# A hybrid GLA and retention trunk on one core: the retention heads' norm moved in part from VectorE to ScalarE, and token sums spread over other steps

## The chip, the cores and the metric

The kernel runs on one core of a Trainium2 chip. The metric is device time in microseconds, the median over runs. The engines that matter are TensorE (PE in the profile, with its weight loads as PEld), VectorE (DVE), ScalarE (ACT), GpSimd (POOL) and SyncE (SP). Each runs its own list of instructions in order and waits for the others by semaphores. SP issues most weight loads from DRAM; POOL issues those that add onto data already loaded, and some small ones.

## The reference

256 tokens of width 2048 pass a gated linear attention layer (4 heads), a retention layer (8 heads) and a final norm, all float32. The change touches the retention layer's norm of each head, the lines from `mu` on:

```python
def retention_mixer(h, positions, w_in, gn_g, gn_b, w_out):
    proj = h @ w_in
    q, k, v, gate = jnp.split(proj, [RET_DK, 2 * RET_DK, 2 * RET_DK + D_INNER], axis=-1)
    ...
    q, k = apply_rotary(q, cos, sin), apply_rotary(k, cos, sin)
    def step(state, inp):
        qb, kb, vb = inp
        scores = jnp.einsum('bhtk,bhsk->bhts', qb, kb) * dmat
        intra = jnp.einsum('bhts,bhsv->bhtv', scores, vb)
        inter = jnp.einsum('bhtk,bhkv->bhtv', qb, state) * xi
        new_state = g_chunk * state + jnp.einsum('bhsk,bhsv->bhkv', kb * zeta, vb)
        return new_state, intra + inter
    ...
    mu = jnp.mean(o, axis=-1, keepdims=True)
    var = jnp.mean(jnp.square(o - mu), axis=-1, keepdims=True)
    o = ((o - mu) * lax.rsqrt(var + EPS)).reshape(B, S, D_INNER).astype(h.dtype)
    o = o * gn_g + gn_b
    return (o * jax.nn.silu(gate)) @ w_out
```

A head's `o` is 256 tokens by 512, `gn_g` and `gn_b` are vectors of 512 for each head, and mean and variance are one number for each token.

## The kernel before

**Weights.** The weights come in pieces of 128x1024 floats (512 KB), each loaded by SP into one of eight `raw` buffers. A piece is split into a high half `hi` (a ScalarE copy to the reduced format that TensorE multiplies fast, L292) and a low half `lo` (VectorE, raw minus high, L293), with four buffers each; the splits run three pieces ahead of their use (`LOOK = 3`). A product is three matmuls: left high by weight high, left high by weight low, left low by weight high (L416, L417 and L418 in the products, L389 and L390 in the query and key steps). TensorE thus waits for a high half from ScalarE, then for a low half from VectorE, which needs the high half.

**Products of a head.** For the value and gate parts of the weights the tokens are taken in two halves, and a scheme of products P1 to P8 on sums of weights and sums of tokens replaces some of the plain ones. Its steps are named in a string for each head; `q` are query and key pieces, `v` and `g` plain value and gate pieces, `P` the products (two weight pieces each, P1a and P1b say), and `z` marks where sums of weights change:

```python
MIXED = "q0 q1 P1 q2 q3 q4 z P5 q5 P6 q6 q7 P2 P3 v4 v5 v6 P7 v7 g4 g5 P8 g6 g7"
SPREAD = "q0 q1 P1 q2 q3 P2 q4 z P5 q5 P6 q6 q7 P3 v4 v5 v6 P7 v7 g4 g5 P8 g6 g7"
```

Heads 2 and 6 follow SPREAD, the odd heads MIXED, heads 0 and 4 take all q first. The weight sums are made in place in `raw`: once both high and low half of a piece of P1, P6 or P3 have been taken, POOL issues a DMA that adds another weight block onto the buffer (L301, `accum_op=ADD`). What P3's pieces become so is P7's weights.

**The head's other work.** `ret_tasks` is a generator that is stepped once at most of the next steps' ends, so a head's rotary, scores, output `o`, norm and transposes run while the next head's products do. Its norm: ScalarE copies `o` out of PSUM while it sums (L1263) and squares it with the mean as bias while it sums (L1267); VectorE adds the mean (which is held negated) and multiplies by `gg` (L1271), turns the variance into an inverse root with an integer start and three Newton steps on 128x2 numbers (`rsqrt`, L514 to L522), multiplies by it and adds `gb` (L1283), and multiplies by the gate `sg` (in the helper `tt`, L1219). TensorE then transposes the result (L725) and ScalarE and VectorE split it into `ogt`. The gate is a SiLU on ScalarE (L1409). Where ScalarE goes from one function's table to that of another set, a table load (ACT_TABLE_LOAD) stands ahead of the instruction.

**Token sums.** For the output projection the sums of tokens over `ogt` are needed. `make_sums` (L473) builds them in five parts in heads 2 and 6, one part at each named step's end, on VectorE and ScalarE; half of them are then spilled to DRAM by two 512 KB DMAs of POOL (`spill_sums`, L456) and read back in heads 3 and 7 (`back_sums`). Before, the parts stand at the ends of q3, P2, q4, P5 and q5, with the spill behind the last.

**The order.** The tile framework's scheduler simulates the program and sets each engine's order from it, with what `keep` marks held in the order of the program and what stands under `tc.high_priority()` preferred. So a change in the code moves other instructions too.

Of the kernel before, what the change touches and what calls it, by code (L numbers as in the profile page):

```python
# [10 lines left out]
F32 = mybir.dt.float32  # L11
# [3 lines left out]
AF = mybir.ActivationFunctionType  # L15
ALU = mybir.AluOpType

P = 128
# [4 lines left out]
GW = 512  # L23
# [147 lines left out]
def kernel(  # L171
# [17 lines left out]
    nc = tc.nc  # L189
# [11 lines left out]
    gn_p = pool("gn", 3)  # L201
    st_p = pool("st", 4)
# [7 lines left out]
    keep = tc.keep_in_program_order  # L210
# [303 lines left out]
    def rsqrt(y, m, n, name):  # L514
        s = st_p.tile([P, 4, n], F32, tag="nw", name=f"{name}_nw")
        a, b = s[:, 0, :], s[:, 1, :]
        nc.vector.tensor_scalar(a.bitcast(I32), m.bitcast(I32), 1, None, ALU.logical_shift_right)
        nc.vector.tensor_scalar(b.bitcast(I32), a.bitcast(I32), -1, 0x5F3759DF, ALU.mult, ALU.add)
        for it in range(3):
            nc.vector.scalar_tensor_tensor(a, b, -0.5, m, ALU.mult, ALU.mult)  # L520
            nc.vector.tensor_tensor(a, a, b, ALU.mult)
            nc.vector.scalar_tensor_tensor(y if it == 2 else b, a, 1.5, b, ALU.add, ALU.mult)  # L522
# [185 lines left out]
    def o_mms(sc, v, ps):  # L708
        for t in range(2):
            steps = [(0, 0)] if t == 0 else [(0, 1), (1, 2)]  # L710
            for n, (s, blk) in enumerate(steps):
                ah = sc[:, 0, blk * P : (blk + 1) * P]
                al = sc[:, 1, blk * P : (blk + 1) * P]
                end = n == len(steps) - 1
                mm(ps[t], ah, v[:, s, 0, :], start=n == 0, stop=False)
                mm(ps[t], ah, v[:, s, 1, :], start=False, stop=False)
                mm(ps[t], al, v[:, s, 0, :], start=False, stop=end)
# [22 lines left out]
    def split_scores(sc32, sc):  # L740
        nc.scalar.activation(sc[:, 0, :], sc32, AF.Copy)
        nc.vector.tensor_tensor(sc[:, 1, :], sc32, sc[:, 0, :].bitcast(F32), ALU.subtract)
# [474 lines left out]
    def ret_tasks(h, qk, r, r2, box):  # L1217

        tt = lambda *x: keep(nc.vector.tensor_tensor(*x))  # L1219
        a = t4_p.tile([P, 4, SEQ], F32, tag="t4", name=f"ra{h}")  # L1220
        b = t4_p.tile([P, 4, SEQ], F32, tag="t4", name=f"rb{h}")
        tb = lambda i, n: trig[:, i : i + 1, :].to_broadcast([P, n, SEQ])
        four = lambda x: x.rearrange("p (a two) t -> p a two t", two=2)
        tt(a, qk, tb(0, 4), ALU.mult)
        dm = sc_p.tile([P, 384], F32, tag="dm", name=f"dm{h}", bufs=1)
        nc.gpsimd.dma_start(dm, dmat[h])
        yield
        tt(four(b)[:, :, 0, :], four(qk)[:, :, 1, :], tb(1, 2), ALU.mult)
        tt(four(b)[:, :, 1, :], four(qk)[:, :, 0, :], tb(1, 2), ALU.mult)
        gg = gn_p.tile([P, GW], F32, tag="gn", name=f"gg{h}")  # L1230
        gb = gn_p.tile([P, GW], F32, tag="gn", name=f"gb{h}")
        nc.gpsimd.dma_start(gg, gn_g[h * GW : (h + 1) * GW].partition_broadcast(P))
        nc.gpsimd.dma_start(gb, gn_b[h * GW : (h + 1) * GW].partition_broadcast(P))
        yield
        tt(four(a)[:, :, 0, :], four(a)[:, :, 0, :], four(b)[:, :, 0, :], ALU.subtract)
        tt(four(a)[:, :, 1, :], four(a)[:, :, 1, :], four(b)[:, :, 1, :], ALU.add)
        yield
        qs = t4_p.tile([P, 2, 2, SEQ], F32R, tag="t4", name=f"rqs{h}")
        ks = t4_p.tile([P, 2, 2, P], F32R, tag="t4", name=f"rks{h}")
        for dst, src in ((qs, a[:, 0:2, :]), (ks, a[:, 2:4, 0:P])):  # L1240
            nc.scalar.activation(dst[:, 0], src, AF.Copy)
            tt(dst[:, 1], src, dst[:, 0].bitcast(F32), ALU.subtract)
        ps = mis_p.tile([P, 384], F32, tag="mis", name=f"rs{h}")
        for kt in range(2):
            mm(ps[:, 256:384], a[:, 2 + kt, P:SEQ], a[:, kt, P:SEQ], start=kt == 0, stop=kt == 1)
        for kt in range(2):
            mm(ps[:, 0:256], ks[:, 0, kt, :], qs[:, 0, kt, :], start=kt == 0, stop=False)
            mm(ps[:, 0:256], ks[:, 0, kt, :], qs[:, 1, kt, :], start=False, stop=False)
            mm(ps[:, 0:256], ks[:, 1, kt, :], qs[:, 0, kt, :], start=False, stop=kt == 1)
        yield  # L1250
        s32 = sc_p.tile([P, 384], F32, tag="s32", name=f"rs32_{h}", bufs=1)
        sc = sc_p.tile([P, 2, 384], F32R, tag="sc", name=f"rsc{h}")
        with tc.high_priority():
            tt(s32, ps, dm, ALU.mult)
            split_scores(s32, sc)
        yield
        po = [mis_p.tile([P, GW], F32, tag="mis", name=f"ro{h}_ps{t}") for t in range(2)]
        o_mms(sc, box["v"], po)
        o = o_p.tile([P, 2, GW], F32, tag="o", name=f"ro{h}")
        mv = st_p.tile([P, 2, 2], F32, tag="mv", name=f"mv{h}")  # L1260
        with tc.high_priority():
            for t in range(2):
                nc.scalar.activation(o[:, t, :], po[t], AF.Copy, accum_out=mv[:, 0, t : t + 1])  # L1263
            nc.vector.tensor_scalar(mv[:, 0, :], mv[:, 0, :], -1.0 / GW, None, ALU.mult)
            for t in range(2):
                mean = mv[:, 0, t : t + 1]
                nc.scalar.activation(po[t], o[:, t, :], AF.Square, bias=mean, accum_out=mv[:, 1, t : t + 1])  # L1267
        yield
        with tc.high_priority():
            for t in range(2):  # L1270
                keep(nc.vector.scalar_tensor_tensor(o[:, t, :], o[:, t, :], mv[:, 0, t : t + 1], gg, ALU.add, ALU.mult))  # L1271
        yield
        m = st_p.tile([P, 2], F32, tag="m", name=f"rm{h}")
        hr = st_p.tile([P, 2], F32, tag="hr", name=f"ra_{h}")
        with tc.high_priority():
            tt(m, mv[:, 1, :], r2, ALU.mult)
            nc.vector.tensor_scalar(m, m, 1.0 / GW, EPS, ALU.mult, ALU.add)
            rsqrt(hr, m, 2, f"rh{h}")
            tt(hr, hr, r, ALU.mult)
        yield  # L1280
        with tc.high_priority():
            for t in range(2):
                keep(nc.vector.scalar_tensor_tensor(o[:, t, :], o[:, t, :], hr[:, t : t + 1], gb, ALU.mult, ALU.add))  # L1283
        yield
        with tc.high_priority():
            for t in range(2):
                tt(o[:, t, :], o[:, t, :], box["sg"][:, t, :], ALU.mult)
        yield
        yield from transpose_out(
            lambda t, j: o[:, t, j * P : (j + 1) * P], (h % 4) * 4, None, ogt, f"rot{h}"  # L1290
        )
# [11 lines left out]
    def ret_head(h):  # L1303
# [8 lines left out]
        r, r2 = r2_[:, 0, :], r2_[:, 1, :]  # L1312
        box = {}
# [21 lines left out]
        def tile_of(key, pool_, shape, dtype, name):  # L1335
            def get():
                if key not in box:
                    box[key] = pool_.tile(shape, dtype, tag=key, name=name)
                return box[key]

            return get

        v = tile_of("v", v_p, [P, 2, 2, GW], F32R, f"rv{h}")
        sg = tile_of("sg", sg_p, [P, 2, GW], F32, f"rsg{h}")
        o = tile_of("o", o_p, [P, 2, GW], F32, f"re{h}")
# [5 lines left out]
        making = make_sums(ogt, f"rsum{h}", sums_apart, "next_s") if h % 4 == 2 else None  # L1351

        def turn(tok):
            n = toks.index(tok)
            if making and tok in ("q3", "P2", "q4", "P5", "q5"):
                next(making)
                if tok == "q5":
                    spill_sums(f"rsum{h}")
            if last and tok == "v7":
                get_resid(f"resid{h}")  # L1360
            if n == drain:
                while tasks:
                    step()
                if mixed:
                    tasks.append(ret_tasks(h, box["qk"], r, r2, box))
            elif n < drain:
                if tok != "q7":
                    step()
            elif mixed:
                if tok not in ("P7", "g4", "g5"):  # L1370
                    step()
                if last and tok == "g7":
                    back_sums(f"rsum{h}")
            elif tok == "P8":
                tasks.append(ret_tasks(h, box["qk"], r, r2, box))
            elif tok in ("g6", "g7"):
                step()
# [211 lines left out]
```

## Time and profile before

| | |
|---|---|
| median of 3 runs | 1388.78 us (1388.77 to 1391.09) |
| the profiled execution's own time | 1387.9 us |
| its span | 1386.1 us |
| mean granted TensorE clock | 0.997 |
| PE busy | 1366.5 us (99%) |
| DVE busy | 1104.1 us (80%) |
| ACT busy | 851.7 us (61%) |
| POOL busy | 145.5 us (10%) |

The span is the trace's, from the first instruction to the last; the run's own time holds 1.8 us more around it. In rows of a timeline the columns are start, duration, engine, line, operation, output<-inputs, shapes, count, and in brackets the idle time before and what ended it. In the groups they are count, busy time, mean ns of one, and idle time before with what ended most of it. Matmul rows overlap: what one costs is read from start to start. Table loads count as ScalarE's busy time.

### The profile page before, as it was taken

How to read it: one execution, taken by the hardware profiler on the slowest of the kernel's cores; microseconds unless marked ns; L12 is line 12 of the kernel's file. 1: busy time of each engine (PE TensorE's matmuls, PEld its weight loads, DVE VectorE, ACT ScalarE, POOL GpSimd, SP SyncE). 2: the span in 40 equal slices, each digit the busy share in tenths (PEclk: the TensorE clock that was granted, in tenths of full speed). 3: DMA queues.
4: the chain of work that ended last, by engine and by line, in shares of the span. 5: the costliest groups of instructions: out<-in, count | busy, mean ns of one | idle time of the engine just before them, and what ended most of it. 6: DMA issues, size and time to landing. Idle time of an engine off the chain costs nothing.

```text
span 1386.1 us, 18745 instructions
## 1 busy us (share of the span) xinstructions
PE 1366.5 (99%) x6736; PEld 1151.6 (83%) x6736; DVE 1104.1 (80%) x1521; ACT 851.7 (61%) x1118; POOL 145.5 (10%) x206
## 2 busy tenths in 40 slices
PE   9999999999999999999999998999999999999997
PEld 7888888888888888887888897888888889788887
DVE  6686795987878887778888896889858898788883
ACT  6576656655567747565666665666556666566662
POOL 1003020110021021001011010101100101010100
PEclk9999999999999999999999999999999999999999
DMA  9765556789659658758897878898898786879881
GB/s 358 248 178 166 175 167 182 168 244 353 192 152 278 182 174 216 286 162 259 278 301 201 254 210 248 208 335 231 247 367 254 193 275 185 257 195 303 236 289 66
DMA packets 85950, 321.36 MB, mean 232 GB/s; under 512 B 9936, under 2 KB 10960, under 8 KB 84320
## 3 DMA queue, kind: packets, MB, share of 16 engines
q1 hardware_dynamic: 66768, 240.55, 49.9%
q0 software_dynamic: 17648, 72.23, 25.3%
q10 hardware_dynamic: 1440, 7.38, 1.4%
q8 instruction: 53, 0.87, 0.2%
q14 instruction: 41, 0.34, 0.1%
HBM read 307.53 MB, written 12.58 MB: 231 GB/s over the span
## 4 chain that ended last, share of the span: by engine, by line
PE 77%; issue 13%; DMA 6%; DVE 2%; POOL 1%; ACT 1%; POOLq 0%; DVEq 0%; SPq 0%; ACTq 0%
DMA raw<-in_w_all 6%; PE rqk_ps L389 5%; PE re_ps L417 5%; PE re_ps L418 5%; PE re_ps L416 5%; PE gqk_ps L389 4%; PE gg_ps L333 3%; PE gv_ps L334 3%; PE gv_ps L333 3%; PE gv_ps L330 3%; PE gg_ps L330 3%; PE gg_ps L334 3%; PE rqk_ps L390 2%; PE ge_ps L417 2%; PE ge_ps L416 2%
## 5 line engine op out<-in xcount | busy, mean ns | idle before, releaser
L293 DVE TENSOR_TENSOR lo<-raw,hi 128x1024 fp32r<-128x1024 f32 (+1 forms) x569 | 687.8, 1222 | 216.4 <-ACT hi L292 203.9
L292 ACT ACTIVATE hi<-raw 128x1024 fp32r<-128x1024 f32 (+1 forms) x569 | 597.8, 1057 | 392.0 <-DMA raw<-in_w_all 65.8
L301 POOL DMA_DIRECT2D raw<-in_w_all x96 | 83.0, 865 | 552.7 <-DVE lo L293 318.9
L417 PE MATMUL re_ps<-lo,xhl 128*128 128x512 f32 x352 | 137.8, 392 | 0.0
L418 PE MATMUL re_ps<-hi,xhl 128*128 128x512 f32 x352 | 136.9, 390 | 0.0
L416 PE MATMUL re_ps<-hi,xhl 128*128 128x512 f32 x352 | 133.1, 392 | 0.0
L389 PE MATMUL rqk_ps<-xhl,hi 128*128 128x512 f32 x360 | 123.3, 397 | 0.0
L390 PE MATMUL rqk_ps<-xhl,lo 128*128 128x256 f32 x360 | 93.7, 282 | 0.0
L389 PEld LDWEIGHTS rqk_ps<-xhl,hi 128*128 128x128 f32 x360 | 66.7, 188 | 13.3
L416 PEld LDWEIGHTS re_ps<-hi,xhl 128*128 128x128 f32 x352 | 66.4, 189 | 13.5
L418 PEld LDWEIGHTS re_ps<-hi,xhl 128*128 128x128 f32 x352 | 66.2, 188 | 13.4
L417 PEld LDWEIGHTS re_ps<-lo,xhl 128*128 128x128 f32 x352 | 66.3, 188 | 13.1
L389 PE MATMUL gqk_ps<-xhl,hi 128*128 128x512 f32 x216 | 76.5, 398 | 0.0
L333 PE MATMUL gg_ps<-lo,xhl 128*128 128x512 f32 x192 | 75.4, 393 | 0.0
L333 PE MATMUL gv_ps<-lo,xhl 128*128 128x512 f32 x192 | 75.2, 392 | 0.0
L330 PE MATMUL gv_ps<-hi,xhl 128*128 128x512 f32 x192 | 75.0, 393 | 0.0
L334 PE MATMUL gv_ps<-hi,xhl 128*128 128x512 f32 x192 | 75.0, 391 | 0.0
L334 PE MATMUL gg_ps<-hi,xhl 128*128 128x512 f32 x192 | 74.9, 390 | 0.0
L330 PE MATMUL gg_ps<-hi,xhl 128*128 128x512 f32 x192 | 74.8, 391 | 0.0
L390 PEld LDWEIGHTS rqk_ps<-xhl,lo 128*128 128x128 f32 x360 | 66.0, 189 | 2.7
L847 POOL TENSOR_TENSOR s<-s,m 128x64 f32<-128x64 f32 x56 | 36.1, 676 | 232.9 <-DVE m L838 223.6
L390 PE MATMUL gqk_ps<-xhl,lo 128*128 128x256 f32 x216 | 59.0, 280 | 0.0
(447 smaller groups left out, 2859.5 us busy)
## 6 DMA issues: line engine op xcount, KB each, us to landing
raw<-in_w_all SPq DMA_DIRECT2D x447, 512.0 KB, 4.9
raw<-in_w_all POOLq DMA_DIRECT2D x96, 512.0 KB, 7.4
resid<-in_x_n SPq DMA_DIRECT2D x2, 1024.0 KB, 10.2
gg<-in_gn_g POOLq DMA_DIRECT2D x8, 256.0 KB, 4.7
resid_x<-resid ACTq DMA_DIRECT2D x1, 2048.0 KB, 8.9
gb<-in_gn_b POOLq DMA_DIRECT2D x8, 256.0 KB, 4.7
gb_resid<-resid_x POOLq DMA_DIRECT2D x1, 2048.0 KB, 11.7
resid_g<-gb_resid ACTq DMA_DIRECT2D x1, 2048.0 KB, 9.7
```

The costliest lines, as they stand in the source:

```text
L292: a = nc.scalar.activation(hi[:, sl], src[:, sl], AF.Copy)
L293: b = nc.vector.tensor_tensor(lo[:, sl], src[:, sl], hi[:, sl].bitcast(F32), ALU.subtract)
L301: nc.gpsimd.dma_start(raws[n], block(key), accum_op=ALU.add)
L330: first_mm = mm(ps, xh, hi[:, q, :], start=kt == 0, stop=False)
L333: mm(ps, xh, lo[:, q, :], start=False, stop=False)
L334: mm(ps, xl, hi[:, q, :], start=False, stop=kt == NKT - 1)
L389: mm(ps[c], wh, rhs[:, kt, :, :], start=kt == 0, stop=False)
L390: mm(ps[c][:, 0, :], wl, rhs[:, kt, 0, :], start=False, stop=False)
L416: mm(ps, xh, hi[:, q, :], start=start, stop=False, **again)
L417: mm(ps, xh, lo[:, q, :], start=False, stop=False, **again)
L418: mm(ps, xl, hi[:, q, :], start=False, stop=stop, **again)
L847: nc.gpsimd.tensor_tensor(dst, dst, side_of(m[:, li, :], z), ALU.add)
```

## The change

*The norm.* The inverse root's start comes from ScalarE. The inverse root, times the token's scale, and its product with the negated mean become scale and bias of a ScalarE pass over each token half of `o` (L1286, `AF.Identity`). `gg`, `gb` and the gate are then applied by three VectorE passes over both token halves at once (128x1024, in the helper `tt`) in place of six of 128x512. *The token sums.* The five parts stand at the ends of q3, q4, q5, P6 and q6, the spill behind q6.

```diff
@@ -1227,10 +1227,10 @@
-        gg = gn_p.tile([P, GW], F32, tag="gn", name=f"gg{h}")
-        gb = gn_p.tile([P, GW], F32, tag="gn", name=f"gb{h}")
-        nc.gpsimd.dma_start(gg, gn_g[h * GW : (h + 1) * GW].partition_broadcast(P))
-        nc.gpsimd.dma_start(gb, gn_b[h * GW : (h + 1) * GW].partition_broadcast(P))
+        gg = gn_p.tile([P, 1, GW], F32, tag="gn", name=f"gg{h}")
+        gb = gn_p.tile([P, 1, GW], F32, tag="gn", name=f"gb{h}")
+        nc.gpsimd.dma_start(gg[:, 0], gn_g[h * GW : (h + 1) * GW].partition_broadcast(P))
+        nc.gpsimd.dma_start(gb[:, 0], gn_b[h * GW : (h + 1) * GW].partition_broadcast(P))
@@ -1266,25 +1266,33 @@
         yield
-        with tc.high_priority():
-            for t in range(2):
-                keep(nc.vector.scalar_tensor_tensor(o[:, t, :], o[:, t, :], mv[:, 0, t : t + 1], gg, ALU.add, ALU.mult))
-        yield
         m = st_p.tile([P, 2], F32, tag="m", name=f"rm{h}")
-        hr = st_p.tile([P, 2], F32, tag="hr", name=f"ra_{h}")
+        hr = st_p.tile([P, 2, 2], F32, tag="hr", name=f"ra_{h}")
+        nw = st_p.tile([P, 4, 2], F32, tag="nw", name=f"rh{h}_nw")
+        a_, b_ = nw[:, 0, :], nw[:, 1, :]
         with tc.high_priority():
             tt(m, mv[:, 1, :], r2, ALU.mult)
             nc.vector.tensor_scalar(m, m, 1.0 / GW, EPS, ALU.mult, ALU.add)
-            rsqrt(hr, m, 2, f"rh{h}")
-            tt(hr, hr, r, ALU.mult)
+            keep(nc.scalar.activation(a_, m, AF.Ln))
+            keep(nc.scalar.activation(b_, a_, AF.Exp, scale=-0.5))
         yield
         with tc.high_priority():
+            nc.vector.scalar_tensor_tensor(a_, b_, -0.5, m, ALU.mult, ALU.mult)
+            tt(a_, a_, b_, ALU.mult)
+            nc.vector.scalar_tensor_tensor(b_, a_, 1.5, b_, ALU.add, ALU.mult)
+            tt(hr[:, 0, :], b_, r, ALU.mult)
+            tt(hr[:, 1, :], hr[:, 0, :], mv[:, 0, :], ALU.mult)
             for t in range(2):
-                keep(nc.vector.scalar_tensor_tensor(o[:, t, :], o[:, t, :], hr[:, t : t + 1], gb, ALU.mult, ALU.add))
+                nc.scalar.activation(
+                    o[:, t, :], o[:, t, :], AF.Identity, bias=hr[:, 1, t : t + 1], scale=hr[:, 0, t : t + 1]
+                )
         yield
         with tc.high_priority():
-            for t in range(2):
-                tt(o[:, t, :], o[:, t, :], box["sg"][:, t, :], ALU.mult)
+            keep(tt(o, o, gg.to_broadcast([P, 2, GW]), ALU.mult))
+            keep(tt(o, o, gb.to_broadcast([P, 2, GW]), ALU.add))
+        yield
+        with tc.high_priority():
+            tt(o, o, box["sg"], ALU.mult)
         yield
@@ -1352,9 +1360,9 @@
-            if making and tok in ("q3", "P2", "q4", "P5", "q5"):
+            if making and tok in ("q3", "q4", "q5", "P6", "q6"):
                 next(making)
-                if tok == "q5":
+                if tok == "q6":
                     spill_sums(f"rsum{h}")
```

The built programs hold 16 table loads on ScalarE before and 38 after: of the 22 more, eight stand ahead of the logarithms, eight ahead of the exponentials and six ahead of SiLUs that follow them. The order on the engines moves at three places.

On POOL in head 2, before: `raw_6830` and `raw_6842` are the buffers that P6's pieces leave to an added block, `raw_7014` and `raw_7051` those of P3, which P7 reads, and `dm` is the next mask of the scores.

```order
L301 DMA raw_6830<-in_w_all 128x1024
L301 DMA raw_6842<-in_w_all 128x1024
L456 DMA rsum_kept<-rsum_t_7301 128x1024
L456 DMA rsum_kept<-rsum_t_7302 128x1024
L301 DMA raw_7014<-in_w_all 128x1024
L301 DMA raw_7051<-in_w_all 128x1024
L1226 DMA dm_8002<-in_dmat 128x384
```

The same place after the change, where `raw_7003` and `raw_7039` are P3's buffers:

```order
L301 DMA raw_6824<-in_w_all 128x1024
L301 DMA raw_6836<-in_w_all 128x1024
L301 DMA raw_7003<-in_w_all 128x1024
L301 DMA raw_7039<-in_w_all 128x1024
L456 DMA rsum_kept<-rsum_t_7342 128x1024
L456 DMA rsum_kept<-rsum_t_7343 128x1024
L1226 DMA dm_7984<-in_dmat 128x384
```

The two spills have moved from ahead of P3's added blocks to behind them; head 6 is the same.

On ScalarE from head 2 into head 3, before: `ro` is head 2's output, `rsg_7109` its gate, `hi_7655` and `hi_7698` are P1's two pieces of head 3 and `hi_7721` is that of q2.

```order
L292 ACTIVATE hi_7635<-raw_7474 128x1024
L1263 ACTIVATE ro_7626,mv_7627<-ro_ps_7615 128x512
L1263 ACTIVATE ro_7626,mv_7627<-ro_ps_7616 128x512
L1267 ACTIVATE ro_ps_7615,mv_7627<-ro_7626,mv_7627 128x512
L1267 ACTIVATE ro_ps_7616,mv_7627<-ro_7626,mv_7627 128x512
L292 ACTIVATE hi_7655<-raw_7507 128x1024
L1409 ACTIVATE rsg_7109<-rsg_7109,r_109 128x512
L1409 ACTIVATE rsg_7109<-re_ps_7084,r_109 128x512
L292 ACTIVATE hi_7698<-raw_7519 128x1024
L292 ACTIVATE hi_7721<-raw_7573 128x1024
```

After the change P1's pieces are `hi_7648` (it stands ahead of these rows) and `hi_7681`, and `hi_7704` is q2's:

```order
L1267 ACTIVATE ro_ps_7604,mv_7615<-ro_7614,mv_7615 128x512
L1417 ACT_TABLE_LOAD
L1417 ACTIVATE rsg_7097<-re_ps_7072,r_109 128x512
L292 ACTIVATE hi_7681<-raw_7507 128x1024
L1417 ACTIVATE rsg_7097<-rsg_7097,r_109 128x512
L1276 ACT_TABLE_LOAD
L1276 ACTIVATE rh_nw<-rm_7639 128x2
L1277 ACT_TABLE_LOAD
L1277 ACTIVATE rh_nw<-rh_nw 128x2
L1286 ACTIVATE ro_7614<-ro_7614,ra_7640 128x512 x2
L292 ACTIVATE hi_7704<-raw_7561 128x1024
```

Three table loads, the logarithm, the exponential and the two passes over `ro` now stand between P1's pieces and q2's high half.

On TensorE in P3 and P2 of head 1, which take turns there, before: `hi_6691` and `lo_6692` are P3's second piece, `hi_6630` is P2's.

```order
L418 MATMUL re_ps_6690<-hi_6630,xhl 128x512
L416 MATMUL re_ps_6547<-hi_6691,sums 128x512
L416 MATMUL re_ps_6749<-hi_6702,xhl 128x512
L417 MATMUL re_ps_6547<-lo_6692,sums 128x512
L418 MATMUL re_ps_6547<-hi_6691,sums 128x512
```

After the change `hi_6653` and `lo_6654` are P3's first piece, `hi_6685` its second and `hi_6604` P2's:

```order
L417 MATMUL re_ps_6542<-lo_6654,sums 128x512
L418 MATMUL re_ps_6542<-hi_6653,sums 128x512
L416 MATMUL re_ps_6542<-hi_6685,sums 128x512
L416 MATMUL re_ps_6684<-hi_6604,xhl 128x512
L417 MATMUL re_ps_6684<-lo_6605,xhl 128x512
L418 MATMUL re_ps_6684<-hi_6604,xhl 128x512
```

The first matmul of P3's second piece stood behind P2's and now stands ahead of them, right behind P3's first piece; head 5 is the same.

## The prediction

> **What bounds the kernel now.** I read the page first, for which engine has no slack.
>
> ```profile
> span 1386.1 us, 18745 instructions
> PE 1366.5 (99%) x6736; PEld 1151.6 (83%) x6736; DVE 1104.1 (80%) x1521; ACT 851.7 (61%) x1118; POOL 145.5 (10%) x206
> ```
>
> TensorE is the bound: 99% busy. VectorE and ScalarE have a fifth and more of the span free, so work added to or taken from them counts only where TensorE waits for them. So the second view is TensorE's waits (total, times, longest, in us), all of them.
>
> ```profile
> PE re_ps L416 <- ACT hi L292: 3.9, 4, 1.3
> PE re_ps L417 <- DVE lo L293: 3.0, 4, 0.8
> PE warm_ps L551 <- POOL warm L549: 1.8, 1, 1.8
> PE gqk_ps L377 <- ACT hi L292: 1.2, 1, 1.2
> PE gbe_ps L416 <- DVE gb_resid L1036: 0.3, 1, 0.3
> PE gae_ps L417 <- DVE lo L293: 0.3, 1, 0.3
> ```
>
> Only the first two are in the retention heads: eight waits, 6.9 us. The timeline puts them at product P7 of heads 2 and 6 (two waits for a high half, two for a low half in each). Head 2:
>
> ```profile
> 836.88 0.39 PE L417 MATMUL re_ps<-lo,xhl 128*128 128x512 f32 x1
> 837.10 0.39 PE L418 MATMUL re_ps<-hi,xhl 128*128 128x512 f32 x1
> 838.79 0.49 PE L416 MATMUL re_ps<-hi,sums 128*128 128x512 f32 x1 [1.30 <-ACT hi L292]
> 842.59 0.50 PE L416 MATMUL re_ps<-hi,sums 128*128 128x512 f32 x1 [1.11 <-ACT hi L292]
> 837.68 1.06 ACT L292 ACTIVATE hi<-raw 128x1024 fp32r<-128x1024 f32 x1 [8.13 <-DMA raw<-in_w_all]
> ```
>
> The wait is 1.30, but from start to start it is 1.69 us, against some 0.23 from one matmul to the next (836.88 to 837.10): a wait costs about 0.2 more than its figure. The last row shows whom TensorE really waits for: ScalarE had been idle 8.13 us for a DMA into the raw buffer. That is the accumulating load that makes P7's weights, issued by POOL:
>
> ```profile
> 819.15 0.85 POOL L301 DMA_DIRECT2D raw<-in_w_all  x1 [0.28 <-DVE lo L293]
> 820.90 0.56 POOL L456 DMA_DIRECT2D rsum_kept<-rsum_t  x1 [0.90 <-DVE rsum_t L489]
> 822.70 0.55 POOL L456 DMA_DIRECT2D rsum_kept<-rsum_t  x1 [1.24 <-DVE rsum_t L489]
> 825.16 1.83 POOL L301 DMA_DIRECT2D raw<-in_w_all  x2 [1.90 <-DVE lo L293]
> raw<-in_w_all POOLq DMA_DIRECT2D x96, 512.0 KB, 7.4
> rsum_kept<-rsum_t POOLq DMA_DIRECT2D x4, 512.0 KB, 9.9
> 830.00:840.00 10.00, 7.99 (x35) 6.04 (x33) 3.17 (x4) 1.06 (x1) 0.00 (x0) 1.00 1.06 308
> 840.00:850.00 10.00, 8.08 (x37) 6.31 (x38) 8.63 (x12) 6.27 (x8) 0.00 (x0) 1.00 0.60 172
> 1200.00:1210.00 10.00, 9.43 (x39) 8.01 (x40) 9.75 (x13) 6.03 (x9) 0.00 (x0) 0.83 0.74 222
> ```
>
> POOL issued P7's first accumulation at 825.16 behind two 512 KB spills, and it landed when the high half began, 837.68: 12.5 us, where the median of these is 7.4. The last three rows (window, us, then PE, PEld, DVE, ACT and POOL busy, granted clock, DMA share, GB/s) add two things: DMA was full (1.06) in that stretch, and after the stall of head 6 the clock fell to 0.83 for ten microseconds, after that of head 2 not.
>
> **The change, part by part.** *Token sums spread out, spill one token later.* In POOL's order the two spills now stand behind P3's two accumulations. These wait for their own low halves, not for the spill, so the issue stays near 825. With the median 7.4 us the data is there at 832.3; TensorE's first matmul of P7 now stands inside v6, eight matmuls (1.8 us) before 837.10, so its high half (1.06) must start by 834.2, a landing of up to 9.1 us. I take 7.4, the row of this very kind; the far end is the 12.5 seen. What goes: 6.9 us of waits plus 8 × 0.22 makes 8.6; and 9.43 busy us at 0.83 are 9.43 × 0.17 = 1.6 of lost clock. Together −10.2. I keep 1.2 back (0.6 a head) for the second half of P7, whose accumulation is issued right behind the first and whose low half is wanted early. Bounds: −10.2 to 0. The spill itself has no reader until the next head's end; the small DMAs queued behind it (a mask, the norm's vectors) are read a head later. The sums' VectorE pieces are the same, only later, hidden by 20% idle.
>
> *The norm.* Durations, from the groups by form (busy, mean ns, idle before):
>
> ```profile
> L293 DVE TENSOR_TENSOR lo<-raw,hi 128x1024 fp32r<-128x1024 f32 x567 | 686.4, 1224 | 215.2 <-ACT hi L292 202.7 <-PE rqk_ps L390 5.3 <-DMA raw<-in_w_all 2.2
> L292 ACT ACTIVATE hi<-raw 128x1024 fp32r<-128x1024 f32 x567 | 596.6, 1058 | 390.6 <-DMA raw<-in_w_all 64.6 <-PE gg_ps L334 49.0 <-PE re_ps L418 42.1
> L1271 DVE SCALAR_TENSOR_TENSOR ro<-ro,mv,gg 128x512 f32<-128x512 f32 x16 | 11.8, 749 | 1.8 <-ACT ro_ps L1267 1.8
> L1283 DVE SCALAR_TENSOR_TENSOR ro<-ro,ra,gb 128x512 f32<-128x512 f32 x16 | 11.3, 748 | 0.1
> L1219 DVE TENSOR_TENSOR ro<-ro,rsg 128x512 f32<-128x512 f32 x16 | 10.7, 687 | 0.0
> L1219 DVE TENSOR_TENSOR ra<-rqk,trig 128x1024 f32<-128x1024 f32 x8 | 9.8, 1221 | 0.0
> L520 DVE SCALAR_TENSOR_TENSOR rh_nw<-rh_nw,rm 128x2 f32<-128x2 f32 x24 | 3.8, 160 | 0.6
> L1399 ACT ACTIVATE rv<-re,r 128x512 fp32r<-128x512 f32 x16 | 11.5, 719 | 7.5 <-DVE re L1447 5.2 <-DVE re L1450 2.1
> 71.17 1.28 ACT L758 ACT_TABLE_LOAD   x1
> 72.47 1.06 ACT L292 ACTIVATE hi<-raw 128x1024 fp32r<-128x1024 f32 x1
> ```
>
> VectorE per head: out go 2 × 0.749 + 2 × 0.748 + 2 × 0.687 = 4.37 and 14 small ones; in come 3 × 1.22 = 3.66 and 7 small ones. At some 0.2 a small one that is −2.1 a head, −17 us in all. ScalarE: 22 more table loads × 1.28 = 28.2, 16 tiny ones × 0.2 = 3.2, 16 passes of 128x512 × 0.72 = 11.5: +43 us, 852 to 895. Neither engine is the bound; both sums are worth 0 by themselves (cover: ScalarE's 390 us idle ahead of high halves, VectorE's 215 ahead of low halves). What counts is where the block of two loads, Ln, Exp and two passes stands in ScalarE's order: ahead of high halves that TensorE needs.
>
> [...]
>
> So I lay the new order over the old times at each hand-over. Heads 0→1 (4→5 is alike):
>
> ```profile
> 745.15 2.21 ACT L292 ACTIVATE hi<-raw 128x1024 fp32r<-128x1024 f32 x2
> 754.11 0.15 DVE L522 SCALAR_TENSOR_TENSOR ra<-rh_nw 128x2 f32<-128x2 f32 x1
> 754.61 0.40 PE L416 MATMUL re_ps<-hi,sums 128*128 128x512 f32 x1
> 754.84 0.39 PE L417 MATMUL re_ps<-lo,sums 128*128 128x512 f32 x1
> ```
>
> From 745.15: high half, load, Ln, high half, load, Exp (2 × (1.05 + 1.28 + 0.20) = 5.1) to 750.2, then three high halves and an eviction (3.65) to 753.9 for P3's first piece; its low half 1.4 to 1.6 later, 755.5 against 754.84: 0.7 late. Its second piece's high half stands behind the two passes (they wait for VectorE's result, about 754.35 as in the row, and end 755.75) and four evictions (1.5): 758.3, and TensorE's first matmul of it, pulled ahead in the new order, wants it six matmuls behind the delayed start, 754.61 + 0.7 + 1.4 = 756.7: 1.6 late. Together 2.3 each, between 0 (four high-half buffers run ahead) and 5.1 (the block in full).
>
> Heads 2→3 (6→7 is alike):
>
> ```profile
> 863.32 1.04 ACT L292 ACTIVATE hi<-raw 128x1024 fp32r<-128x1024 f32 x1
> 873.22 0.62 PE L389 MATMUL rqk_ps<-xhl,hi 128*128 128x512 f32 x2
> 929.84 1.06 ACT L292 ACTIVATE hi<-raw 128x1024 fp32r<-128x1024 f32 x1
> 940.98 0.39 PE L417 MATMUL rae_ps<-lo,ogt 128*128 128x512 f32 x1
> ```
>
> Squares end about 864.2 with the first high half now ahead of them; Silu's load to 865.5; Silu, high half and Silu to 867.8; load, Ln, load, Exp (2.96) to 870.75; five small VectorE steps (1.1) to 871.85; two passes (1.35) to 873.2; q2's high half to 874.25 against 873.22: 1.05 late, and 0.35 more for its low half behind a wide multiplication. Together 1.4 each, between 0 and 3. Heads 3 and 7 into the output: from 929.84 the same steps and a third load bring the needed low half to 941.2 against 940.98: 0.3 each, between 0 and 1. Heads 1→2 and 5→6 keep a few tenths of lead: 0, up to 1 each. Sum: 2 × (2.3 + 1.4 + 0.3) = +8.0, between 0 and 20.
>
> Net: −10.2 + 1.2 + 8.0 = −1.0. The profiled execution took 1387.9 us with its span of 1386.1, so it becomes 1386.9; the median of the runs shown, 1388.78, is 0.9 above the profiled one, so **1387.8 us**. Its own range, with the new stalls between 5 and 11.5, is 1384.5 to 1391.5. A change of 0.2%, 2.8 us, is about what a measurement of this kernel tells from none, so this is no difference (1386.0 to 1391.6).
>
> **Rivals.** *Faster: the block is absorbed.* The high halves run up to three pieces ahead and ScalarE has 390 us idle before them; then the new stalls are about 2 us and nothing is left at P7: −10.2 + 2 = −8.2, 1380.6. Against it: at the hand-overs the hand-laid order leaves leads of tenths only. It decides once the new stalls are under 6.2.
>
> *Slower: ScalarE's block holds all eight hand-overs.* The table loads are a fixed 2.6 to 3.8 us each; if each of the eight loses 2.3 us, the new stalls are 18.4 and the net is −10.2 + 1.2 + 18.4 = +9.4, 1398.2. For it: every loss found is a chain across three engines, and TensorE's clock fell to 0.83 after one stall. Against: two of the four kinds of hand-over come out at 0.3 or less. It decides from 11.8 of new stalls.
>
> *The P7 stall stays.* DMA is full (1.06) in 830 to 840 by weight loads too, so the accumulation may be late though it is ahead in POOL's queue. Then only the new stalls count: +8.0, 1396.8. Against: 12.5 is far from the median of 7.4, and the two spills (9.9 median) are what is special to heads 2 and 6.
>
> [...]
>
> **How the numbers follow.** Forecast 0.36, absorbed 0.28, all hand-overs 0.19, stall stays 0.13, doubled switch 0.04. The forecast's own range spills a little over both bounds: 0.05 faster, 0.04 slower, 0.27 within. So faster 0.28 + 0.05 = 0.33, same 0.27, slower 0.19 + 0.13 + 0.04 + 0.04 = 0.40. For 8 in 10 the range must reach both neighbours: low 1379.5 (absorbed, a microsecond under), high 1399 (all hand-overs, a microsecond over).
>
> **What would show it.** Right: TensorE's waits for high and low halves at P7 of heads 2 and 6 gone or under 1 us a head; no clock under 0.9 near 1200; 38 table loads of 1.28; VectorE 17 us less busy, ScalarE 43 more; new waits of 1 to 2 us at P3 of heads 1 and 5 and q2 of heads 3 and 7. Wrong: P7's high half still waiting for a DMA past 835; waits in heads 2 and 6 at their start; or no new waits at all. What would upset the sum most is a scheduler-made order in which one late high half delays a buffer and with it later loads, which rows of before cannot show.

## The result and the profile after

The changed kernel takes 1394.0 us (median of 7 runs, 1392.43 to 1395.79) against 1388.77 us of the kernel before: a ratio of 1.0038, 95% interval 1.0026 to 1.0049. It is slower by 5.2 us. The forecast was 1387.8 us, no difference.

The page of the changed kernel, its first rows (span; busy time, share and instructions of each engine):

```profile
span 1392.1 us, 18716 instructions
PE 1369.3 (98%) x6736; PEld 1149.8 (83%) x6736; DVE 1091.4 (78%) x1441; ACT 889.4 (64%) x1172; POOL 145.7 (10%) x206
```

VectorE has 12.7 us less to do, ScalarE 37.7 us more, and the span is 6.0 us longer. The waits of TensorE (total, times, longest) say where; left out are two at the kernel's start that are there before too (`warm`, `gqk`) and one of 0.2 us:

```profile
PE rqk_ps L389 <- ACT hi L292: 3.0, 2, 1.5
PE re_ps L416 <- ACT hi L292: 2.7, 4, 1.0
PE rae_ps L417 <- DVE lo L293: 1.1, 2, 0.9
PE rbe_ps L417 <- DVE lo L293: 1.1, 2, 0.8
PE rae_ps L416 <- ACT hi L292: 0.9, 1, 0.9
PE rbe_ps L416 <- ACT hi L292: 0.7, 1, 0.7
PE re_ps L417 <- DVE lo L293: 0.6, 2, 0.3
PE rqk_ps L390 <- DVE lo L293: 0.5, 2, 0.3
PE rae_ps L416 <- DVE resid L1036: 0.4, 1, 0.4
```

None of these stands at P7 any more, and there are new places: `rqk` is a head's queries and keys (q2), `re` P3 and its neighbours, and `rae` and `rbe` are the two halves of the output projection. In the kernel before, TensorE waited at none of these.

**P7.** POOL in head 2, and ScalarE's high half of P7's first piece:

```profile
827.71 0.86 POOL L301 DMA_DIRECT2D raw<-in_w_all  x1 [4.33 <-DVE lo L293]
829.01 0.85 POOL L301 DMA_DIRECT2D raw<-in_w_all  x1 [0.45 <-DVE lo L293]
830.05 0.56 POOL L456 DMA_DIRECT2D rsum_kept<-rsum_t  x1 [0.19 <-issue]
834.82 1.06 ACT L292 ACTIVATE hi<-raw 128x1024 fp32r<-128x1024 f32 x1 [1.58 <-DMA raw<-in_w_all]
```

From issue to high half it is now 7.1 us (827.71 to 834.82), where it was 12.5. ScalarE still waits for that load, 1.58 us, but TensorE doesn't wait for ScalarE. The window 1200 to 1220 shows a granted clock of 1.00 in the trace; the 0.83 of before is gone with its stall.

**The hand-overs.** Heads 0→1, ScalarE and then TensorE:

```profile
745.62 1.28 ACT L1276 ACT_TABLE_LOAD   x1
748.09 1.28 ACT L1277 ACT_TABLE_LOAD   x1
753.54 1.52 ACT L1286 ACTIVATE ro<-ro,ra 128x512 f32<-128x512 f32 x2 [0.62 <-DVE ra L1219]
754.97 1.18 ACT L1334 ACTIVATE rqk_h<-rqk_ps 128x256 f32<-128x256 f32 x4
756.02 2.02 ACT L292 ACTIVATE hi<-raw 128x1024 fp32r<-128x1024 f32 x2
754.02 0.40 PE L416 MATMUL re_ps<-hi,sums 128*128 128x512 f32 x1
754.69 0.50 PE L417 MATMUL re_ps<-lo,sums 128*128 128x512 f32 x1 [0.28 <-DVE lo L293]
757.14 0.50 PE L416 MATMUL re_ps<-hi,sums 128*128 128x512 f32 x1 [1.04 <-ACT hi L292]
```

P3's second high half starts at 756.02, behind the two passes and the evictions; its first matmul follows P3's first piece and so waits. From start to start 0.67 and 1.42 us against 0.23: 1.6 us are lost. Heads 2→3:

```profile
862.48 1.28 ACT L1417 ACT_TABLE_LOAD   x1
866.04 1.28 ACT L1276 ACT_TABLE_LOAD   x1
867.33 0.20 ACT L1276 ACTIVATE rh_nw<-rm 128x2 f32<-128x2 f32 x1
867.55 1.28 ACT L1277 ACT_TABLE_LOAD   x1
870.06 1.52 ACT L1286 ACTIVATE ro<-ro,ra 128x512 f32<-128x512 f32 x2 [1.01 <-DVE ra L1219]
871.49 2.94 ACT L292 ACTIVATE hi<-raw 128x1024 fp32r<-128x1024 f32 x3
870.67 0.39 PE L418 MATMUL re_ps<-hi,xhl 128*128 128x512 f32 x1
872.58 1.21 PE L389 MATMUL rqk_ps<-xhl,hi 128*128 128x512 f32 x4 [1.52 <-ACT hi L292]
```

Three loads, the passes, and only then q2's high half: 1.91 us from start to start, 1.7 lost, and 0.4 more for the low half. Each load is followed at once (866.04 to 867.33, 1.29 us).

**What was not foreseen.** Into the output projection TensorE waits three more times, here 13 us and 60 us behind the hand-over of head 3:

```profile
953.30 0.39 PE L416 MATMUL rae_ps<-hi,rsum 128*128 128x512 f32 x1
954.55 0.50 PE L417 MATMUL rae_ps<-lo,ogt 128*128 128x512 f32 x1 [0.85 <-DVE lo L293]
1001.62 0.49 PE L416 MATMUL rae_ps<-hi,ogt 128*128 128x512 f32 x1 [0.86 <-ACT hi L292]
1002.54 0.50 PE L416 MATMUL rae_ps<-hi,rsum 128*128 128x512 f32 x1 [0.42 <-DVE resid L1036]
940.00:954.00 14.00, 13.47 (x63) 10.60 (x61) 14.00 (x15) 8.61 (x10) 2.12 (x4) 1.00 0.63 154
953.90 0.87 POOL L301 DMA_DIRECT2D raw<-in_w_all  x1 [0.84 <-DVE raw L287]
991.61 1.76 POOL L301 DMA_DIRECT2D raw<-in_w_all  x2 [1.39 <-DVE raw L287]
```

The same window and the same two issues of the kernel before:

```profile
940.00:954.00 14.00, 14.00 (x68) 11.58 (x67) 14.00 (x17) 8.84 (x10) 3.12 (x4) 1.00 0.64 154
949.93 0.85 POOL L301 DMA_DIRECT2D raw<-in_w_all  x1 [0.28 <-issue]
987.69 1.76 POOL L301 DMA_DIRECT2D raw<-in_w_all  x2 [1.38 <-DVE raw L287]
```

In these 14 us VectorE is busy without a gap (14.00) in both kernels: here it, and not TensorE, has no slack. The new norm gives it the three wide passes later, so the weight sums (L287) and low halves behind them come later, and POOL issues the accumulating loads 4.0 and 3.9 us later than before, though TensorE starts the output at the same time in both (932.40 and 932.36) and had lost only 0.4 us at the hand-over. The wait at 1001.62 is the second end of this.

By place, in us lost from start to start against 0.23 a matmul:

| place | foreseen | measured |
|---|---|---|
| P7 of heads 2 and 6 | −8.6, and 1.2 kept back | −8.6, nothing left |
| clock after head 6's stall | −1.6 | −1.7 |
| P3 of heads 1 and 5 | 2 × 2.3 | 2 × 1.6 |
| q2 of heads 3 and 7 | 2 × 1.4 | 2 × 2.1 |
| first low half of the output, both halves | 2 × 0.3 | 2 × 0.4 |
| output, 13 us on, both halves | none | 2 × 1.0 |
| output, 60 us and 24 us on | none | 1.0 + 0.7, 0.8 |
| heads 1 and 5, behind P3 | none | 0.6 + 0.4, 0.4 |

That is −10.3 + 8.2 + 5.9 = +3.8 of the 6.0 us by which the span grew; the other 2.2 are in gaps of under 0.4 us each, which weren't followed.

### The profile page after: what moved, and what is told of

The parts are those of the page before. It is cut to its first block, busy times and chain, and to the rows that moved or that the text cites. A ratio compares the mean times of both kernels' runs of the same rounds, so it can differ in the third digit from the quotient of the medians.

```text
span 1392.1 us, 18716 instructions
## 1 busy us (share of the span) xinstructions
PE 1369.3 (98%) x6736; PEld 1149.8 (83%) x6736; DVE 1091.4 (78%) x1441; ACT 889.4 (64%) x1172; POOL 145.7 (10%) x206
## 4 chain that ended last, share of the span: by engine, by line
PE 85%; DMA 4%; DVE 4%; ACT 3%; issue 3%; POOL 0%; DVEq 0%; SPq 0%; POOLq 0%; ACTq 0%
PE re_ps L417 7%; PE re_ps L418 7%; PE re_ps L416 6%; PE rqk_ps L389 5%; DMA raw<-in_w_all 4%; PE gqk_ps L389 4%; PE gg_ps L333 3%; PE gv_ps L334 3%; PE gv_ps L333 3%; PE gv_ps L330 3%; PE gg_ps L330 3%; PE gg_ps L334 3%; PE rqk_ps L390 2%; PE ge_ps L417 2%; PE ge_ps L416 2%
## 5 line engine op out<-in xcount | busy, mean ns | idle before, releaser
L416 PEld LDWEIGHTS re_ps<-hi,xhl 128*128 128x128 f32 x352 | 65.8, 188 | 15.3 <-ACT hi L292 1.4
```

What stands on the lines that cost most here:

```text
L416: mm(ps, xh, hi[:, q, :], start=start, stop=False, **again)
```

## The experiments

**The sums alone, and the norm alone.** The kernel before with only the sums' tokens changed, as below, and the changed kernel with the same lines put back:

```diff
-            if making and tok in ("q3", "P2", "q4", "P5", "q5"):
+            if making and tok in ("q3", "q4", "q5", "P6", "q6"):
                 next(making)
-                if tok == "q5":
+                if tok == "q6":
```

> The kernel before with only the token sums' five parts and their spill moved (q3, q4, q5, P6, q6), the norm untouched; in its order the two spills stand behind P3's added blocks. Theory A (the stall at P7 came from the spills ahead of P3's accumulating loads; the norm's change costs what was lost): the four waits at P7 go in heads 2 and 6 and nothing comes in their place, -8.6 us of waits and -1.6 of clock, about 1378.6 us. Rival (those loads land late because DMA is full with weights, and the changed kernel hides it since its heads run later): the waits stay at least by half, 1384 to 1389 us.

> The changed kernel with the token sums' parts back at q3, P2, q4, P5, q5 and the spill asked for behind q5. Its order still has the two spills behind P3's added blocks, so this keeps the spill's new place in POOL's queue and undoes only the spreading of VectorE's and ScalarE's parts. Theory A (the queue's order is what counts): no waits at P7, as the changed kernel, 1394 us within 2. Rival (the spreading of the parts is what counts): the P7 waits are back, +8.6 to +10.2 us, 1402 to 1404 us.

Measured: 1378.9 us for the sums alone, ratio 0.9935 (0.9923 to 0.9947), and 1393.94 us for the norm alone, 1.0046 (1.0033 to 1.0058). So the P7 stall cost about what it seemed to, some 9 us, and the norm's edit costs 15 us on top of the sums (1378.9 to 1394.0). The second run holds a surprise: the norm's edit by itself makes the scheduler put the spills behind the accumulating loads (in head 2 these are issued at 826.32 and 827.62, the spills at 828.66 and 831.60), so the changed kernel would have lost the P7 stall without the other edit. The waits of TensorE in the sums' kernel that are left in the retention layer are one group (the scores of heads 2 and 6, waiting for the high half of the rotated keys, which ScalarE copies at L1241):

```profile
PE rs L1247 <- ACT rks L1241: 1.6, 2, 0.9
```

**The spills' place alone.** To separate POOL's order from the spreading of the parts, the parts stay where they were and only the spills are held behind P3's added blocks. The first form holds the order of all accumulating loads, the second only from q4 to P3 of heads 2 and 6. This is the second; in both, the spills' own DMAs are marked with `keep` too:

```diff
-            nc.gpsimd.dma_start(raws[n], block(key), accum_op=ALU.add)
+            made = nc.gpsimd.dma_start(raws[n], block(key), accum_op=ALU.add)
+            if cur.get("hold"):
+                keep(made)
...
+            keep(nc.gpsimd.dma_start(
...
+            ))
...
-                if tok == "q5":
-                    spill_sums(f"rsum{h}")
+            if making and tok in ("q4", "P3"):
+                cur["hold"] = tok == "q4"
+            if making and tok == "P3":
+                spill_sums(f"rsum{h}")
```

> The kernel before with nothing changed but the place of the two spills: they are asked for behind P3 and held behind P3's two added blocks in POOL's order; the token sums' parts stay at q3, P2, q4, P5, q5. Theory A (the queue's order makes the P7 stall): the P7 waits go, 1377 to 1381 us as in the run with the parts moved (1378.9). Rival (the parts had to be spread): 1386 to 1389 us.

> As the run with the spills behind P3's added blocks, but the order is held only for the loads issued from q4 to P3 of heads 2 and 6, so that nothing else of the kernel before moves (the run before it also held the gated linear attention's loads in program order and lost 25 us there). Theory A (the queue's order makes the P7 stall): 1377 to 1381 us. Rival (the parts had to be spread): 1386 to 1389 us.

Measured: 1402.92 us, ratio 1.0114 (1.0098 to 1.0129), for the first, 1378.31 us, 0.9930 (0.9917 to 0.9942), for the second. The first missed its expectation, but not at P7, where its trace has no wait above 0.4 us: holding all the loads in the order of the program cost the gated linear attention waits of 3 us (`gae` and `gbe`), and clock with them (0.66 from 275 to 285 us, 0.70 from 322 to 332). These are waits of TensorE in the first form:

```profile
PE gae_ps L416 <- ACT hi L292: 6.0, 2, 3.2
PE re_ps L416 <- ACT hi L292: 3.5, 5, 1.4
PE gbe_ps L416 <- ACT hi L292: 3.2, 1, 3.2
```

The second form is the clean one. Its POOL and ScalarE rows in head 2:

```profile
823.60 0.87 POOL L301 DMA_DIRECT2D raw<-in_w_all  x1 [4.97 <-DVE lo L293]
825.44 1.44 POOL L458 DMA_DIRECT2D rsum_kept<-rsum_t  x2
829.88 1.06 ACT L292 ACTIVATE hi<-raw 128x1024 fp32r<-128x1024 f32 x1 [1.94 <-DMA raw<-in_w_all]
```

Issue to high half is 6.3 us, half of the 12.5 of before, with the same parts at the same steps. The second load of the pair landed 10.3 us after its issue, where it was 15.3. The gain, 0.7%, is that of the sums alone, so the order of one queue is enough for all of it.

**The table loads.** Four forms of the changed kernel take the norm's edit apart. In the first, no_loads, the root is made by the integer start and three Newton steps on VectorE; the ScalarE pass and the wide passes stay:

```diff
-            keep(nc.scalar.activation(a_, m, AF.Ln))
-            keep(nc.scalar.activation(b_, a_, AF.Exp, scale=-0.5))
+            rsqrt(hr[:, 0, :], m, 2, f"rh{h}")
...
```

The second, idle_loads, adds to it a logarithm and an exponential that nothing reads:

```diff
...
+            keep(nc.scalar.activation(un[:, 0, :], m, AF.Ln))
+            keep(nc.scalar.activation(un[:, 1, :], un[:, 0, :], AF.Exp, scale=-0.5))
             rsqrt(hr[:, 0, :], m, 2, f"rh{h}")
```

The third, detour, is the changed kernel with copies in place of the two functions. It leaves out the root: the start of its Newton step is the constant 0.05, so it serves for timing alone. The fourth, ln_old_passes, keeps logarithm, exponential and one Newton step and has the six VectorE passes of before in place of the ScalarE pass and the three wide ones. The lines of detour:

```diff
-            keep(nc.scalar.activation(a_, m, AF.Ln))
-            keep(nc.scalar.activation(b_, a_, AF.Exp, scale=-0.5))
+            keep(nc.scalar.activation(a_, m, AF.Copy, scale=0.0))
+            keep(nc.scalar.activation(b_, a_, AF.Copy, bias=0.05))
```

> The changed kernel with the inverse root by integer start and three Newton steps on VectorE as before, so without logarithm, exponential and the 22 table loads; the ScalarE pass and the wide VectorE passes stay. Theory A1 (the table loads and the detour over ScalarE are the new stalls): the waits at P3 of heads 1 and 5 (1.6 us each) and at q2 of heads 3 and 7 (2.1 each) go, and with them a part of those in the output, 1382 to 1387 us. Theory A2 (the ScalarE pass and the wide passes are what holds): the waits stay, 1392 to 1395 us.

> The kernel without logarithm and exponential (1380.6 us), to which a logarithm and an exponential of the variance are added whose results nothing reads: the 22 table loads are back on ScalarE, but VectorE's inverse root waits for nothing of ScalarE. Theory L (the loads hold ScalarE, and high halves queue behind them): most of the 13 us return, 1388 to 1394 us. Theory D (the chain VectorE, ScalarE, VectorE is what is late; the loads matter only as a part of it): 1380 to 1384 us.

> The changed kernel with two small ScalarE copies in the place of the logarithm and the exponential (the inverse root's start is then a constant, so the norm isn't computed): the same chain over three engines and the same passes, 16 table loads as before. Theory L: as without logarithm and exponential, 1379 to 1383 us. Theory D: 1388 to 1394 us.

> The changed kernel with logarithm, exponential and one Newton step, but the passes over the output as before (six VectorE ones of 128x512, no ScalarE pass). Theory L with the loads alone: within 3 us of the changed kernel, 1391 to 1396 us. If the ScalarE pass (1.4 us a head on the engine that the loads fill) and its place in the chain are half of it: 1384 to 1389 us. If the wide passes were the loss: 1379 to 1382 us.

| form | loads | root waits for ScalarE | ScalarE pass | us | ratio to before |
|---|---|---|---|---|---|
| changed | 38 | yes | yes | 1394.0 | 1.0038 |
| idle_loads | 38 | no | yes | 1387.96 | 0.9999 (0.9990 to 1.0007) |
| ln_old_passes | 36 | yes | no | 1385.74 | 0.9976 (0.9966 to 0.9986) |
| no_loads | 16 | no | yes | 1380.61 | 0.9950 (0.9937 to 0.9962) |
| detour | 16 | yes | yes | 1379.95 | 0.9938 (0.9926 to 0.9951) |

Without the loads next to nothing is lost, neither by the chain over three engines nor by the new passes: detour, which has both, is 1.1 us above the sums alone and no_loads 1.7, and the intervals of all three overlap. (no_loads came out 1.4 us under the range expected of it.) With the loads, 7.4 us are lost even where nothing waits for them (idle_loads against no_loads), mostly by high and low halves that stand behind them; the other 6.0 come only when the root, and behind it the ScalarE pass, must wait for them too. In ln_old_passes, where the ScalarE pass is gone, they are gone as well, though TensorE there waits 1.2 us ahead of the transposes in each of two heads. Neither theory alone was right: the loads are the cause, and half of their price is paid through the chain. The waits show the two halves apart. TensorE in idle_loads:

```profile
PE re_ps L416 <- ACT hi L292: 2.0, 2, 1.0
PE re_ps L417 <- DVE lo L293: 1.4, 2, 0.7
PE rae_ps L416 <- ACT hi L292: 1.0, 1, 1.0
PE rae_ps L418 <- DVE ogt L733: 0.6, 1, 0.6
```

P3's waits stay, 2.0 us lost in each of heads 1 and 5, but those of `rqk`, q2 of heads 3 and 7, are gone: there the passes start at 869.63, without idle time before them, and q2's high half no longer comes late.

The wait 60 us into the output goes with the loads too. Counted from the output's first matmul, POOL issues the two accumulating loads (at 987.69 and 991.61 above) 55.3 us on in the kernel before and 59.2 us on in the changed one. Without the loads it is 56.5 (no_loads) and 56.4 (detour), and TensorE doesn't wait for a high half there; with them it is 57.4 (ln_old_passes) and 59.2 (idle_loads), and it waits 0.84 and 0.97 us. So without the loads only about 1 of the 3.9 us of lateness is left. The short wait for `resid` right behind (0.4 us) stays in all four, so that one isn't the loads' doing.

**The pass on VectorE.** In the changed kernel, the pass by scale and bias moved back:

```diff
-                nc.scalar.activation(
-                    o[:, t, :], o[:, t, :], AF.Identity, bias=hr[:, 1, t : t + 1], scale=hr[:, 0, t : t + 1]
-                )
+                keep(nc.vector.tensor_scalar(
+                    o[:, t, :], o[:, t, :], hr[:, 0, t : t + 1], hr[:, 1, t : t + 1], ALU.mult, ALU.add
+                ))
```

> The changed kernel with the pass by scale and bias on VectorE (two of 128x512) in place of ScalarE; logarithm, exponential, 38 table loads and the wide passes stay. If the ScalarE pass is what makes 1394 out of the 1386 that the loads with the old passes take: 1384 to 1388 us. If it is the wide passes (later transposes): 1391 to 1395 us.

Measured: 1387.51 us, ratio 0.9993 (0.9982 to 1.0004), so 6.5 us under the changed kernel, with all its 38 loads. The waits at q2 are gone here as well, though VectorE has more to do:

```profile
PE re_ps L417 <- DVE lo L293: 2.6, 2, 1.3
PE re_ps L416 <- ACT hi L292: 2.6, 5, 0.9
```

**By heads.** The norm of before stands under the condition, the changed one under the other branch; in the first run the heads with it are 3 and 7, in the second (`h % 4 in (0, 2)`) the even ones:

```diff
+        if h % 4 == 3:
...
+        else:
...
```

> The changed kernel with the norm of before in heads 3 and 7 alone, whose norm runs while the output projection's first products do. Theory A3 (the waits of the output stretches, 0.4 at its start, 1.0 at some 13 us, 1.7 and 0.8 at 60 and 25 us, come from this norm, by VectorE full of wide passes and then by accumulating loads issued late): they go, -5.3 us, about 1388.7 us. Rival (they come from the lateness that the hand-over 2 to 3 and 6 to 7 left behind): they stay, 1393 to 1395 us.

> The changed kernel with the norm of before in heads 0, 2, 4 and 6, so that the new norm is left in the odd heads, two of which run into the output. By the sum of places: the waits at P3 of heads 1 and 5 (1.6 each), at q2 of heads 3 and 7 (2.1 each) and the small ones near 775 us (1.4) go, about -9, 1385 us, and those in the output (6.2) stay. Rival (the output's waits are lateness handed down from the earlier hand-overs): they shrink too, 1379 to 1382 us.

Measured: 1387.76 us, ratio 0.9999 (0.9990 to 1.0008), and 1382.27 us, 0.9960 (0.9945 to 0.9974). The first gives back 6.2 us, against 5.3 by the sum of the output's places, and in its trace no wait is left in the output: those stalls come from the norm of heads 3 and 7, not from lateness handed down, for the waits at q2 ahead of them are still there (1.5 us each). The second gives back 11.7 us, more than the 9 of its places and nearer to the rival's time than to the 1385 us expected; but in the output only the 0.8 of the second half goes with them, and the rest stays. By the ratios the two give back 0.0117 together against the 0.0103 that the norm costs, and the intervals cover the difference, so it isn't shown that any of it was paid once for both.

**One step further.** The sums' kernel with the head's own work stepped at P7 and not at v6 in heads 2 and 6, for the 1.6 us of the scores:

```diff
-                if tok not in ("P7", "g4", "g5"):
+                if tok not in (("v6" if h % 4 == 2 else "P7"), "g4", "g5"):
```

> The kernel before with only the token sums moved (1378.9 us), and in heads 2 and 6 the head's own work is stepped at P7 and not at v6, so that the scores stand one step later. There the scores' matmuls waited 0.9 us for ScalarE (1.0 more from start to start) in each of the two heads: these waits go, about -1.7 us, 1377 us; if the step only moves the wait to where the head's output is needed, 1378 to 1380 us.

Measured: 1378.06 us, ratio 0.9927 (0.9914 to 0.9940). The wait is gone in head 6 and stays in head 2 (0.9 us); against the sums alone (0.9935) the intervals overlap. The sums' edit without the norm's is thus the version to keep: 0.65% under the kernel before, 1.1% under the changed one.

## Why the prediction was wrong

The forecast named no difference, and the kernel is slower, clear of the interval. By its own chances slower was the likelier (0.40 against 0.27), and the time lies within its wide range; but none of its rivals, and not its own sum, describes where the time was lost.

- **P7 held.** The waits went, and with them the lost clock. The 1.2 us kept back for P7's second half weren't needed. The reason given, two spills ahead of the accumulating loads in POOL's queue, is shown by the run that changed only that order. What the text had wrong is whose doing it was: it credited the sums' edit, but the norm's edit moves the spills too.
- **The hand-overs held in sum, not one by one**: 8.0 foreseen, 8.2 found. That they agree is luck, as two errors cancel. P3 was over-estimated by 0.7 in each of its two heads (the first low half 0.4 late and not 0.7, the second high half 1.2 and not 1.6), q2 under-estimated by as much (the ScalarE passes began at 870.06, 0.84 us before TensorE wanted the high half at 870.67 + 0.23, where the working had 1.4 us, 871.85 against 873.22).
- **The failed step is the sum "2 × (2.3 + 1.4 + 0.3) = +8.0"**, which ends each loss at its hand-over and so puts all that follows at nothing. The runs put 5.9 us more in its place, behind the hand-overs: 4.5 in the output and 1.4 in heads 1 and 5. Its ground was "both sums are worth 0 by themselves", with a cover of 390 us on ScalarE and 215 us on VectorE. These are sums over the whole span; in the 14 us behind head 3 VectorE has no idle time at all, in the kernel before too, and a window there would have shown it. A full VectorE alone isn't enough: no_loads also has 14.00 busy us from 936 to 950 and TensorE doesn't wait there. It took work that came late into such a stretch. It wasn't caught up, and it was handed on through the accumulating loads, which POOL issued 4 us later, to TensorE 60 us on. The prediction's last sentence named a late high half that delays later loads as the danger, but gave it no term. With these 5.9 and without the 1.2 the forecast's own sum gives +3.7 in place of −1.0; the 2.2 us in small gaps stay open.
- **The rivals.** "All eight hand-overs" had the sign but not the place: heads 1→2 and 5→6 show no wait at their hand-over. "The block is absorbed" and "the P7 stall stays" fall by the traces. No run shows the doubled switch (0.04 of the chances): at 866.04 to 867.33 the logarithm starts 1.29 us after its load of 1.28 does, and in the trace before it is 1.30 from a load's start to the next instruction (71.17 to 72.47). The idle time ahead of the eight loads is 0.1 us in all in the row below, from the groups of the changed kernel.

```profile
L1276 ACT ACT_TABLE_LOAD x8 | 10.3, 1283 | 0.1
```

- **The busy times** were over-estimated: VectorE has 12.7 us less to do and not 17, ScalarE 37.7 more and not 43. Neither enters the sum.
- **The loads' price** was taken at 28 us of ScalarE's time, off the path, plus the hand-overs. Measured by taking them away they cost 13.4 us (1394.0 to 1380.61): nearly half of their busy time reached the end, on an engine that is busy 64% of the span.

## What to carry to other kernels

Idle time of an engine over the whole span is no cover; look at the window in which the moved work lands, and, where an engine is full there, follow the delay through what that engine releases (buffers, accumulating loads) until it is used, not just to the first wait. A function whose table isn't loaded held up, by its load of 1.28 us, every instruction behind it in that engine's order, and again what waited for its result: here, next to a busy copy engine, the small roots were 13.4 us cheaper as a dozen tiny VectorE instructions a head. And before two edits are credited with one effect, look at the order each makes alone: here one queue's order was worth some 9 us, and either edit moved it.

## What the runs showed of the hardware

The same stall of under 2 us cost clock in one run and none in another. The wait at q2 of head 3 is 1.91 us from start to start in the changed kernel and in the run with the norm of before in heads 3 and 7, and the windows of ten microseconds from it read (us; PE, PEld, DVE, ACT and POOL busy; granted clock; DMA share; GB/s), first the changed kernel:

```profile
870.00:880.00 10.00, 8.24 (x42) 6.42 (x41) 8.41 (x9) 7.71 (x9) 1.12 (x2) 1.00 0.70 179
```

and the other run:

```profile
870.00:880.00 10.00, 8.23 (x35) 6.45 (x34) 8.43 (x8) 6.85 (x8) 1.13 (x2) 0.83 0.70 183
```

The clock is 0.83 in one and 1.00 in the other. Windows of one microsecond show the drop of the other run as a clock of 0.50:

```profile
875.00:876.00 1.00, 1.00 (x4) 0.81 (x4) 1.00 (x2) 0.81 (x1) 0.56 (x1) 0.50 0.98 115
876.00:877.00 1.00, 1.00 (x4) 0.88 (x4) 1.00 (x2) 0.00 (x0) 0.00 (x0) 0.50 0.78 266
```

The microsecond ahead of these reads 0.68 and the one behind 0.62: 1.7 us of clock lost in four, which at 0.50 is some 3.4 us of lowered clock, an estimate from these four windows. The run with the norm alone shows 0.83 at this place too, and at q2 of head 7, with a stall of the same length, all three runs show 1.00. In the 3 us from 871 to 874, ahead of the drop, TensorE was busy for 1.2; in the changed kernel, whose clock stays at 1.00, it was busy for 1.27 there. What makes the clock fall in some places and not in others isn't shown by these runs.

The other number is the queue's: the same accumulating load of 512 KB took 12.5 us from issue to use behind two spills of 512 KB in its queue and 6.3 us ahead of them, and the load behind it 15.3 and 10.3 us to its landing. The DMA engines were full in both stretches: the share was 1.06 before, and in the run with the spills held behind it is this row's 1.03 (the last but one number):

```profile
823.00:833.00 10.00, 10.00 (x55) 8.67 (x54) 8.19 (x9) 4.54 (x6) 2.84 (x4) 1.00 1.03 260
```

So with the DMA engines as full, a place ahead of the spills brings these loads in sooner. The place isn't all that sets the time: with the sums alone the first load is ahead of the spills too, and took 9.1 us to land.
